# ScalarE and VectorE in hardware loops, GpSimd casting eight rows at a time, in a DMA-bound fused low-rank linear layer

## Chip, cores, metric

One core of a Trainium2 chip. The metric is device time in microseconds (us), median over executions. Every execution also has a span (first to last instruction of the kernel); the time is about 1.3 us above the span.

## The reference, cut

```python
x_flat = x.reshape(-1, in_dim)                 # x: 16 x 2048 x 256, float32
y = x_flat @ W                                 # W: 256 x 256
lora_out = ((x_flat @ lora_A) * lora_E) @ lora_B   # rank 16
y = y + scale * lora_out
```

Input and output are 33.55 MB each. The kernel folds the low-rank part into one weight matrix, so the work on x is one 256 x 256 product in bf16.

## The kernel before, the parts that matter

x stands in four chunks of 64 rows on each of 128 partitions. Three chunks have a place each in SBUF; the fourth is loaded over the first when that has been stored. One queue, issued by SyncE, carries all loads (`L`, chunk, first row, end) and stores (`S`) in this order:

```python
ORDER = [("A",), ("L",0,0,8), ("L",0,8,24), ("L",0,24,40), ("L",0,40,64),
         ("L",1,0,32), ("L",1,32,64), ("L",2,0,16), ("L",2,16,64),
         ("S",0,0,40), ("S",0,40,64), ("L",3,0,32), ("L",3,32,64),
         ("S",1,0,64), ("S",2,0,64), ("S",3,0,64)]
HELD = (2, 16)                 # GpSimd casts this row of chunk 2, and all behind it, only
HOLDERS = (("S", 0, 0, 40),)   # after this store has landed
```

A group is four rows (64 groups in all). GpSimd casts it to bf16, TensorE (PE) transposes it as pairs of bf16 words, VectorE (DVE) copies the transposed data out of PSUM, PE multiplies by the folded weights, ScalarE (ACT) copies the result over the rows that x came from. PE runs a hardware loop; the other engines' programs are written out:

```python
# GpSimd
for g in range(N_GROUPS):
    ... # waits for the load, and for the holder
    if g >= NS:
        gpsimd.wait_ge(s_turned, g - NS + 1)
    gpsimd.tensor_copy(out=stage[g % NS][:], in_=home(c)[:, b:b + CG, :]).then_inc(s_stage[g % UNROLL], 1)
# ScalarE
for g in range(N_GROUPS):
    scalar.wait_ge(s_y, g + 1)
    scalar.copy(out=home(c)[:, b:b + CG, :], in_=psum_y[g % NY][:]).then_inc(s_free[(g + NY) % UNROLL], 1)
    if g in ends:
        scalar.drain().then_inc(s_done, 1)      # releases a store
# VectorE
for g in range(N_GROUPS):
    vector.wait_ge(s_turned, g + 1)
    vector.tensor_copy(out=xt[g % NX][:], in_=psum_xt[g % NT][:].bitcast(BF16)).then_inc(s_xt[g % UNROLL], 1)
# PE
with tensor.Fori(0, N_GROUPS // UNROLL):
    for i in range(UNROLL):
        turn(i + 1, i)
        multiply(i)
# [cut: set-up, the end]
```

Of the kernel before, what the change touches and what calls it, by code (L numbers as in the profile page):

```python
# [7 lines left out]
P = 128  # L8
FP32 = mybir.dt.float32
BF16 = mybir.dt.bfloat16  # L10
# [3 lines left out]
ROWS = 64  # L14
N_CHUNKS = 4
N_HOMES = 3

ORDER = [
    ("A",),
    ("L", 0, 0, 8),  # L20
    ("L", 0, 8, 24),
    ("L", 0, 24, 40),
    ("L", 0, 40, 64),
    ("L", 1, 0, 32),
    ("L", 1, 32, 64),
    ("L", 2, 0, 16),
# [13 lines left out]
WARM_UP = 2  # L40

CG = 4
GPC = ROWS // CG
N_GROUPS = N_CHUNKS * GPC

NS, NX, NT, NY = 2, 2, 2, 2

UNROLL = 4
# [3 lines left out]
def kernel(  # L52
# [20 lines left out]
    y_chunks = out_flat.rearrange("(c p b) m -> c p b m", p=P, b=ROWS)  # L73

    sbuf, psum, sem = nc.alloc_sbuf_tensor, nc.alloc_psum_tensor, tc.alloc_semaphore
    homes = [sbuf(f"home{h}", [P, ROWS, K], FP32) for h in range(N_HOMES)]
    stage = [sbuf(f"stage{i}", [P, CG, K], BF16) for i in range(NS)]
    xt = [sbuf(f"xt{i}", [P, CG, P * KT], BF16) for i in range(NX)]
    ident = sbuf("ident", [P, P], FP32)

    w_sb = sbuf("w_sb", [P, KT, M], FP32)
    a_sb = sbuf("a_sb", [P, KT, R], FP32)
    b_sb = sbuf("b_sb", [R, M], FP32)
    e_sb = sbuf("e_sb", [R, 1], FP32)
    ate = sbuf("ate", [R, KT, P], FP32)
    weff = sbuf("weff", [P, KT, M], BF16)
    psum_xt = [psum(f"psum_xt{i}", [P, CG, P], FP32) for i in range(NT)]
    psum_y = [psum(f"psum_y{i}", [P, CG, M], FP32) for i in range(NY)]
# [8 lines left out]
    stored = {op: sem(f"stored_{op[1]}_{op[2]}") for op in ORDER if op in waited}  # L97
    stored_rest = nc.alloc_semaphore("stored_rest")
    n_rest = sum(op[0] == "S" and op not in waited for op in ORDER)
    ends = sorted((c * ROWS + e) // CG - 1 for kind, c, s, e in (op for op in ORDER if op[0] == "S"))  # L100
    s_ident = sem("ident_made")
    s_pe_set_up = sem("pe_set_up")
    s_ate = sem("ate_made")
    s_stage = [sem(f"staged{i}") for i in range(UNROLL)]
    s_turned = sem("turned")
    s_xt = [sem(f"xt_made{i}") for i in range(UNROLL)]
    s_y = sem("multiplied")
    s_free = [sem(f"y_free{i}") for i in range(UNROLL)]
    s_done = sem("rows_done")

    def home(c):
        return homes[c % N_HOMES]

    sync, gpsimd, scalar, vector, tensor = nc.sync, nc.gpsimd, nc.scalar, nc.vector, nc.tensor

# [19 lines left out]
    def sync_program():  # L135
        for n, op in enumerate(ORDER):
            if op[0] == "A":
                a = lora_A.rearrange("(q t) r -> q t r", t=KT)
                ins = sync.dma_start(out=a_sb[:], in_=a).then_inc(set_up_loaded["a"], 16)
                opening.append(ins.ins.name)  # L140
                continue
            kind, c, s, e = op
            at_home = home(c)[:, s:e, :]
            if kind == "L":
                for st in stored:
                    if st[1] == c - N_HOMES and st[2] < e and s < st[3]:
                        sync.wait_ge(stored[st], 16)
                ins = sync.dma_start(out=at_home, in_=x_chunks[c, :, s:e, :]).then_inc(loaded[op], 16)
                if n == 1:
                    opening.append(ins.ins.name)  # L150
            else:
                sync.wait_ge(s_done, ends.index((c * ROWS + e) // CG - 1) + 1)
                sync.dma_start(out=y_chunks[c, :, s:e, :], in_=at_home).then_inc(stored.get(op, stored_rest), 16)

    def gpsimd_program():
        gpsimd.memset(ident[:], 0.0).then_inc(s_ident, 1)  # L156
        gpsimd.wait_ge(s_ident, 1)
        gpsimd.affine_select(  # L158
            out=ident[:],
            in_=ident[:],  # L160
            compare_op=ALU.not_equal,
            fill=1.0,
            base=0,
            pattern=[[-1, P]],
            channel_multiplier=1,
        ).then_inc(s_ident, 1)
        for g in range(N_GROUPS):
            c, b = g // GPC, g % GPC * CG
            for op, landed in loaded.items():
                if op[1:3] == (c, b):  # L170
                    gpsimd.wait_ge(landed, 16)
            if (c, b) == HELD:
                for op in HOLDERS:
                    gpsimd.wait_ge(stored[op], 16)
            if g >= NS:
                gpsimd.wait_ge(s_turned, g - NS + 1)  # L176
            gpsimd.tensor_copy(out=stage[g % NS][:], in_=home(c)[:, b:b + CG, :]).then_inc(s_stage[g % UNROLL], 1)  # L177

        gpsimd.wait_ge(s_turned, N_GROUPS - NS + 1)
        gpsimd.drain().then_inc(s_stage[N_GROUPS % UNROLL], 1)  # L180

    def scalar_program():
        for name, to, of in (
            ("w", w_sb, W.rearrange("(q t) m -> q t m", t=KT)),
            ("b", b_sb, lora_B),
            ("e", e_sb, lora_E[:, None]),
        ):
            ins = scalar.dma_start(out=to[:], in_=of).then_inc(set_up_loaded[name], 16)
            opening.append(ins.ins.name)
        for g in range(N_GROUPS):  # L190
            c, b = g // GPC, g % GPC * CG
            scalar.wait_ge(s_y, g + 1)
            scalar.copy(out=home(c)[:, b:b + CG, :], in_=psum_y[g % NY][:]).then_inc(s_free[(g + NY) % UNROLL], 1)  # L193
            if g in ends:
                scalar.drain().then_inc(s_done, 1)  # L195

    def vector_program():
        vector.wait_ge(set_up_loaded["e"], 16)
        vector.wait_ge(s_pe_set_up, 1)
        vector.tensor_scalar(  # L200
            out=ate[:],
            in0=psum_y[0][:R, :KT, :P],
            scalar1=e_sb[:],
            scalar2=float(scale),
            op0=ALU.mult,
            op1=ALU.mult,
        ).then_inc(s_ate, 1)
        for g in range(N_GROUPS):
            vector.wait_ge(s_turned, g + 1)
            vector.tensor_copy(out=xt[g % NX][:], in_=psum_xt[g % NT][:].bitcast(BF16)).then_inc(s_xt[g % UNROLL], 1)  # L210
            if g == 0:
                vector.wait_ge(set_up_loaded["w"], 16)
                vector.wait_ge(s_pe_set_up, 2)
                vector.tensor_add(out=weff[:], in0=w_sb[:], in1=psum_y[1][:, :KT, :]).then_inc(s_free[0], 1)  # L214
                vector.drain().then_inc(s_free[1], 1)

    def tensor_program():
        def turn(i, result=None):
            words = stage[i % NS][:].bitcast(FP32)
            staged = s_stage[i % UNROLL]  # L220
            for b in range(CG):
                if b == 0:
                    tensor.wait_ge(staged, 1)
                if b == CG - 1 and result is not None:
                    tensor.wait_ge(s_free[result % UNROLL], 1)
                ins = tensor.transpose(psum_xt[i % NT][:, b, :], words[:, b, :], ident[:])  # L226
                if b == 0:
                    ins.then_inc(staged, -1)
            ins.then_inc(s_turned, 1)

        def multiply(i):
            turned, free = s_xt[i % UNROLL], s_free[i % UNROLL]
            for b in range(CG):
                for t in range(KT):
                    if b == t == 0:
                        tensor.wait_ge(turned, 1)
                    ins = tensor.matmul(  # L237
                        psum_y[i % NY][:, b, :],
                        xt[i % NX][:, b, t::KT],
                        weff[:, t, :],  # L240
                        start=(t == 0),
                        stop=(t == KT - 1),
                    )
                    if b == 0:
                        ins.then_inc((turned, free)[t], -1)
            ins.then_inc(s_y, 1)

        tensor.wait_ge(s_ident, 2)
        for i in range(WARM_UP):
            tensor.matmul(psum_y[1][:, :2, :], ident[:], ident[:, None, :].to_broadcast([P, 4, P]), start=True, stop=True)  # L250
        tensor.wait_ge(set_up_loaded["a"], 16)
        for t in range(KT):
            ins = tensor.transpose(psum_y[0][:R, t, :P], a_sb[:, t, :], ident[:])  # L253
        ins.then_inc(s_pe_set_up, 1)
        turn(0)
        tensor.wait_ge(set_up_loaded["b"], 16)
        tensor.wait_ge(s_ate, 1)
        for t in range(KT):
            ins = tensor.matmul(psum_y[1][:, t, :], ate[:, t, :], b_sb[:], start=True, stop=True)  # L259
        ins.then_inc(s_pe_set_up, 1)  # L260
        assert N_GROUPS % UNROLL == 0 and all(UNROLL % n == 0 for n in (NS, NX, NT, NY))
        with tensor.Fori(0, N_GROUPS // UNROLL):
            for i in range(UNROLL):
                turn(i + 1, i)
                multiply(i)

    def wait_for_stores(nc):
        nc.sync.wait_ge(stored_rest, 16 * n_rest).then_inc(stored_rest, -16 * n_rest)
# [44 lines left out]
```

## Time and profile before

| | before |
|---|---|
| time, median of 3 | 161.36 us (161.30 to 161.37) |
| time of the profiled execution | 162.84 us, span 161.5 us |
| data moved by the queue of x and y | 67.13 MB |

The profiled execution is 1.48 us slower than the median of the timed ones.

From the page of the kernel before: the span, the DMA engines' mean busy share and rate in 40 slices of the span, and the queues (packets, bytes, share of 16 engines' span).

```profile
span 161.5 us, 2024 instructions
...
DMA  7999999999999997998999999799799799699690
GB/s 253 405 438 452 402 452 446 446 406 446 394 548 414 402 390 337 477 467 371 420 459 440 406 446 536 319 519 471 308 503 487 308 503 503 292 503 503 292 519 16
...
q1 hardware_dynamic: 2304, 67.13, 97.2%
...
q14 instruction: 3, 0.02, 0.0%
```

The data queue is busy 97.2% of the span: the kernel is bound by its DMA engines. The last slice holds almost no traffic. Three packets of the queue that the page calls instruction (q14; instruction fetches below) share the engines with it: 8192 bytes and 0.31 us each in the trace, at 80.95, 86.49 and 102.70 us, each starting 3 to 4 ns before a data packet of its engine ends.

The issues of SyncE, the DMA queue's own row of the timeline, kernel before (start, length in us, engine, line, what, count):

```profile
0.00 0.38 SPq L139 DMA_DIRECT2D a_sb<-in_lora_A_dram  x1
0.43 4.95 SPq L148 DMA_DIRECT2D home<-in_x_dram  x8
27.66 9.87 SPq L153 DMA_DIRECT2D out_dram<-home  x2
75.94 7.69 SPq L148 DMA_DIRECT2D home<-in_x_dram  x2
83.68 35.34 SPq L153 DMA_DIRECT2D out_dram<-home  x3
```

Every store is issued long before the engines reach it: the first at 27.66 us, behind eight loads that keep the engines busy until about 62 us, the last at 119 us, behind two older ones that keep them busy until about 139 us.

The stages of the kernel before (busy us of each engine, granted clock, DMA share, rate):

```profile
core 0: us, PE busy (x) PEld busy (x) DVE busy (x) ACT busy (x) POOL busy (x), PEclk, DMA share, GB/s
...
27.00:60.00 33.00, 31.52 (x289) 29.12 (x288) 16.60 (x24) 24.18 (x25) 23.86 (x23) 1.00 1.04 438
60.00:76.00 16.00, 0.96 (x9) 0.61 (x7) 0.69 (x1) 1.71 (x2) 0.00 (x0) 0.64 0.93 398
...
80.00:118.00 38.00, 37.58 (x337) 34.37 (x335) 18.67 (x27) 28.73 (x29) 25.94 (x25) 0.98 1.04 448
118.00:161.50 43.50, 0.00 (x0) 0.00 (x0) 0.00 (x0) 0.63 (x1) 0.00 (x0) 0.55 0.90 390
```

PE stands still by design while GpSimd is held (60 to 76 us) and has finished 43 us before the end. The page's chain of waits nevertheless names PE:

```profile
DMA 36%; PE 34%; POOL 1%; ACT 1%; issue 0%; SPq 0%; ACTq 0%; POOLq 0%
```

That chain follows releases. PE released stores that then stood in the queue, so its 34% are not time that a faster PE would save.

### The profile page before, as it was taken

Reading aid. Unit: us, or ns where it says so; the run is one execution under the profiler, and the core shown is the slowest. Engines: PE = TensorE matmul, PEld = TensorE weight load, DVE = VectorE, ACT = ScalarE, POOL = GpSimd, SP = SyncE. Lnnn points to the kernel's source line nnn. Section 1 sums busy time; section 2 is a strip of 40 time slices with the busy share of each in tenths; the row PEclk is TensorE's granted clock in tenths of the full one; section 3 lists DMA queues with packets and bytes.
Section 4 is the critical chain, followed back from the end, with each engine's and each line's share of the span. In section 5 each row is a group of like instructions: output and inputs, shape, how many; then the busy total and the mean of one; then the engine's idle time right before and its main releaser. Section 6 shows DMA issues by size and latency. Waiting matters only on the chain.

```text
span 161.5 us, 2024 instructions
## 1 busy us (share of the span) xinstructions
PE 95.4 (59%) x782; PEld 83.4 (52%) x782; DVE 45.4 (28%) x66; ACT 66.1 (41%) x65; POOL 66.9 (41%) x70
## 2 busy tenths in 40 slices
PE   2988999969999990000899999999910000000000
PEld 1347999959999990000789989999900000000000
DVE  0141555535555550000155555555400000000000
ACT  3003677747777772000157777777730000000000
POOL 1516768577778840001578777788200000000000
PEclk9975999999999999555599999999996555555555
DMA  7999999999999997998999999799799799699690
GB/s 253 405 438 452 402 452 446 446 406 446 394 548 414 402 390 337 477 467 371 420 459 440 406 446 536 319 519 471 308 503 487 308 503 503 292 503 503 292 519 16
DMA packets 2515, 67.43 MB, mean 418 GB/s; under 512 B 448, under 2 KB 464, under 8 KB 592
## 3 DMA queue, kind: packets, MB, share of 16 engines
q1 hardware_dynamic: 2304, 67.13, 97.2%
q10 hardware_dynamic: 208, 0.28, 0.6%
q14 instruction: 3, 0.02, 0.0%
HBM read 33.85 MB, written 33.55 MB: 417 GB/s over the span
## 4 chain that ended last, share of the span: by engine, by line
DMA 36%; PE 34%; POOL 1%; ACT 1%; issue 0%; SPq 0%; ACTq 0%; POOLq 0%
DMA out_dram<-home 30%; PE psum_y L237 22%; PE psum_xt L226 12%; DMA home<-in_x_dram 6%; POOL stage L177 1%; ACT home L193 1%; ACTq L195 0%; SPq L308 0%; POOLq L176 0%; SPq L272 0%
## 5 line engine op out<-in xcount | busy, mean ns | idle before, releaser
L193 ACT COPY home<-psum_y 128x1024 f32<-128x1024 f32 x64 | 64.8, 1012 | 50.5 <-PE psum_y L237 50.5
L177 POOL CAST stage<-home 128x1024 bf16<-128x1024 f32 x64 | 66.2, 1042 | 44.8 <-DMA out_dram<-home 17.5
L237 PE MATMUL psum_y<-weff,xt 128*128 128x256 bf16 x512 | 69.6, 281 | 0.0
L210 DVE COPY xt<-psum_xt 128x1024 bf16<-128x1024 bf16 x64 | 44.3, 692 | 63.4 <-PE psum_xt L226 63.4
L237 PEld LDWEIGHTS psum_y<-weff,xt 128*128 128x128 bf16 x512 | 51.8, 101 | 6.5
L226 PE MATMUL psum_xt<-ident,stage 128*128 128x128 f32 x260 | 41.4, 283 | 19.3 <-POOL stage L177 19.0
L226 PEld LDWEIGHTS psum_xt<-ident,stage 128*128 128x128 f32 x260 | 31.5, 146 | 22.1 <-issue 20.7
L250 PE MATMUL psum_y<-ident 128*128 128x512 f32 x4 | 3.7, 1078 | 2.9 <-POOL ident L158 2.9
L250 PEld LDWEIGHTS psum_y<-ident 128*128 128x128 f32 x4 | 1.2, 324 | 3.9 <-POOL ident L158 2.9
L200 DVE TENSOR_SCALAR ate<-psum_y,e_sb 16x256 f32<-16x256 f32 x1 | 0.5, 472 | 6.9 <-PE psum_y L253 6.9
L193 ACT ACT_TABLE_LOAD x1 | 1.3, 1283 | 2.1 <-SPq L272 2.1
L259 PE MATMUL psum_y<-b_sb,ate 16*128 16x256 f32 x4 | 1.1, 400 | 0.0
L156 POOL MEMSET ident<- 128x128 f32 x1 | 0.2, 205 | 1.7 <-SPq L272 1.7
L253 PEld LDWEIGHTS psum_y<-ident,a_sb 128*16 128x16 f32 x2 | 0.2, 114 | 1.2 <-issue 1.2
L214 DVE TENSOR_TENSOR weff<-w_sb,psum_y 128x512 bf16<-128x512 f32 x1 | 0.7, 687 | 0.4 <-PE psum_y L259 0.4
L259 PEld LDWEIGHTS psum_y<-b_sb,ate 16*128 16x128 f32 x4 | 0.7, 184 | 0.2 <-issue 0.2
L158 POOL TENSOR_SCALAR_AFFINE_SELECT ident<-ident 128x128 f32<-128x128 f32 x1 | 0.3, 293 | 0.2 <-POOL ident L156 0.2
L253 PE MATMUL psum_y<-ident,a_sb 128*16 128x128 f32 x2 | 0.4, 273 | 0.0
L294 POOL MEMSET const-float32-0.0<- 128x1 f32 x1 | 0.1, 99 | 0.2 <-issue 0.2
L294 POOL MEMSET const-bfloat16-1.0<- 128x1 bf16 x1 | 0.1, 103 | 0.0
L294 POOL MEMSET const-uint8-127<- 128x1 uint8 x1 | 0.1, 103 | 0.0
L294 POOL MEMSET const-float32-1.0<- 128x1 f32 x1 | 0.1, 99 | 0.0
## 6 DMA issues: line engine op xcount, KB each, us to landing
home<-in_x_dram SPq DMA_DIRECT2D x4, 4096.0 KB, 25.1
home<-in_x_dram SPq DMA_DIRECT2D x3, 2048.0 KB, 13.8
home<-in_x_dram SPq DMA_DIRECT2D x1, 6144.0 KB, 58.9
out_dram<-home SPq DMA_DIRECT2D x1, 5120.0 KB, 48.3
home<-in_x_dram SPq DMA_DIRECT2D x1, 3072.0 KB, 20.7
out_dram<-home SPq DMA_DIRECT2D x1, 3072.0 KB, 46.0
home<-in_x_dram SPq DMA_DIRECT2D x1, 1024.0 KB, 5.4
w_sb<-in_W_dram ACTq DMA_DIRECT2D x1, 256.0 KB, 3.0
```

What stands on the lines that cost most here:

```text
L158: gpsimd.affine_select(out=ident[:], in_=ident[:], compare_op=ALU.not_equal, fill=1.0, base=0, pattern=[[-1, P]], channel_multiplier=1,).t ...
L177: gpsimd.tensor_copy(out=stage[g % NS][:], in_=home(c)[:, b:b + CG, :]).then_inc(s_stage[g % UNROLL], 1)
L193: scalar.copy(out=home(c)[:, b:b + CG, :], in_=psum_y[g % NY][:]).then_inc(s_free[(g + NY) % UNROLL], 1)
L200: vector.tensor_scalar(out=ate[:], in0=psum_y[0][:R, :KT, :P], scalar1=e_sb[:], scalar2=float(scale), op0=ALU.mult, op1=ALU.mult,).then_in ...
L210: vector.tensor_copy(out=xt[g % NX][:], in_=psum_xt[g % NT][:].bitcast(BF16)).then_inc(s_xt[g % UNROLL], 1)
L214: vector.tensor_add(out=weff[:], in0=w_sb[:], in1=psum_y[1][:, :KT, :]).then_inc(s_free[0], 1)
L226: ins = tensor.transpose(psum_xt[i % NT][:, b, :], words[:, b, :], ident[:])
L237: ins = tensor.matmul(psum_y[i % NY][:, b, :], xt[i % NX][:, b, t::KT], weff[:, t, :], start=(t == 0), stop=(t == KT - 1),)
L250: tensor.matmul(psum_y[1][:, :2, :], ident[:], ident[:, None, :].to_broadcast([P, 4, P]), start=True, stop=True)
L253: ins = tensor.transpose(psum_y[0][:R, t, :P], a_sb[:, t, :], ident[:])
L259: ins = tensor.matmul(psum_y[1][:, t, :], ate[:, t, :], b_sb[:], start=True, stop=True)
L294: nc = _bacc.Bacc("TRN2", target_bir_lowering=False, num_devices=1)
```

## The change

The intent: shorter instruction streams, by assumption with fewer instruction fetches on busy DMA engines, and fewer waits for counts that grow. ACT's and DVE's copies become hardware loops, which needs one `ring` tensor in place of three homes and waits for the constant 1, with PE taking the counts down again. GpSimd casts eight rows at once. The larger stage buffers are paid for by laying the set-up weights in `stage[1]`. Stores are released by PE's count, two groups later. One small copy stands ahead of ACT's loop, so that the loading of the activation table goes with it; before it took 1.28 us at 2.05 us, under the line of the group copies (L193). The diff, cut to its core:

```diff
+CAST = 2 * CG
-    homes = [sbuf(f"home{h}", [P, ROWS, K], FP32) for h in range(N_HOMES)]
-    stage = [sbuf(f"stage{i}", [P, CG, K], BF16) for i in range(NS)]
+    ring = sbuf("ring", [P, RING, K], FP32)
+    stage = [sbuf(f"stage{i}", [P, CAST, K], BF16) for i in range(NS)]
+    spare = stage[1][:].bitcast(FP32)...    # w_sb, b_sb, ate live here at the start
 # SyncE
-                sync.wait_ge(s_done, ends.index((c * ROWS + e) // CG - 1) + 1)
+                sync.wait_ge(s_done, (c * ROWS + e) // CG + NY)
 # GpSimd: 32 casts for 64
+            if n == 1:
+                gpsimd.wait_ge(s_weff, 1)
+            if n >= NS:
+                gpsimd.wait_ge(s_room, n - NS + 1)
+            gpsimd.tensor_copy(out=stage[n % NS][:], in_=rows(c, b, b + CAST)).then_inc(s_stage[n % NS], 1)
 # ScalarE
-        for g in range(N_GROUPS): ...
+        scalar.copy(out=one[:], in_=ident[:, :1])
+        for n in (RING, N_CHUNKS * ROWS - RING):
+            with scalar.Fori(0, n // (UNROLL * CG)) as lap:
+                for i in range(UNROLL):
+                    scalar.wait_ge(s_y[i], 1)
+                    to = ring[:, bass.ds(lap * (UNROLL * CG) + i * CG, CG), :]
+                    scalar.copy(out=to, in_=psum_y[i % NY][:]).then_inc(s_free[(i + NY) % UNROLL], 1)
 # VectorE
+        with vector.Fori(0, N_GROUPS // UNROLL):
+            for i in range(UNROLL):
+                g = i + 1
+                vector.wait_ge(s_turned[g % UNROLL], 1)
+                vector.tensor_copy(...)
 # PE, in multiply(i)
+            updates = {(0, 1): (s_xt[i % UNROLL], -1), (1, 0): (s_free[i % UNROLL], -1),
+                       (1, 1): (s_turned[i % UNROLL], -1), (2, 0): (s_y[(i - NY) % UNROLL], -1),
+                       (2, 1): (s_done, 1), (3, 1): (s_y[i % UNROLL], 1)}
 # [cut: set-up of the counts, the end]
```

## The prediction

> **What bounds the kernel now.** The DMA engines. The page's queue table gives the data queue (loads of x, stores of y) 97.2% of 16 engines' span, 67.13 MB in 161.5 us; the table of stages shows a DMA share near 1 and 437 to 448 GB/s from 12 to 60 us and from 80 to 118 us, then stores alone. Compute is off the path: PE is busy 59%, ACT 41%, POOL 41%, DVE 28%; PE stands still from about 62 to 77 us (GpSimd waits for the first store by design), and compute ends at 118.6 us. The chain of waits names PE for 34% because it follows releases, but the store released at 27.7 us then took 48.3 us behind queued loads, and the last store is issued at 119 us with older stores to move until about 139 us. PE's pace (1.31 us per four-row group) has 20 us of slack at the end, the first store some 30.
>
> Within the DMA the path is the slowest of the 16 engines. Single packets in the trace: each engine moves about 27 GB/s back to back, but 13 finish between 158.3 and 159.0 us, the others at 159.4, 159.9 and 161.07. The straggler was 1.2 us behind the first engine from 11 us on, 1.95 after 62 us, 2.8 after the load that ends at 93 us. That last step holds an instruction fetch: the instruction queue moves three 8 KB packets, at 80.95, 86.49 and 102.70 us, 0.31 us each. The second and the slowed x packet after it (0.54 us over normal) cost one engine 0.85 us, which fits the straggler's step.
>
> **What the change does.** Data transfers and their order stay. ACT's and DVE's streams shrink to loops (64 copies become 4 per lap), POOL's casts from 64 to 32. [...] PE already loops here without fetches. I expect all three gone, at worst one left (GpSimd's, late).
>
> It adds: a first cast of 8 rows (estimate 2.05 us for 1.04), so PE starts about 1 us later; a second cast waiting for the folded weights, whose scratch space is now in its buffer; 64 address updates plus branches on ACT ([...]within its 0.3 us idle[...]); stores released two groups (2.6 us) later by PE's count. All inside slack, worth zero. The small copy moves the 1.28 us table load, off the path either way.
>
> **Sum.** Straggler minus its fetch: -0.85 us. The ramp and the slow patch at 59 to 62 us (all engines about 0.8 us late) stay.
>
> Predicted: 160.6 us, range 159.6 to 161.6. Chances: faster by over 2% 0.03, within 2% 0.95, slower by over 2% 0.02.
>
> **What shows it right or wrong.** Right: no instruction packets inside the span; data queue still 67.13 MB; spread of engine ends from 2.8 to about 2 us; stores issued later but landings unmoved; PE groups of 1.3 to 1.5 us. Wrong: instruction packets from loop branches; a hole in the DMA row where a store came late.
>
> **What would make it wrong.** The straggler's lag may come from the profile or chance, so that timed runs gain nothing; [...]ACT's address updates would have to eat 20 us of slack to matter.

The sum has one term, -0.85 us, set against the 161.36 us of the time table: 160.51 us, put as 160.6 us. That a loop needs no fetches rests on PE's loop alone; beyond that it was assumption.

## The result, and the profile after

| | before | after |
|---|---|---|
| first measurement, median | 161.44 us (161.30 to 161.65, 6) | 162.06 us (161.77 to 162.67, 6) |
| ratio of the fast runs, 95% interval | | 1.0041 (1.002 to 1.0061) |
| three repeats, ratio | | 0.9984 (0.9947 to 1.0022), 0.9999 (0.9977 to 1.0021), 1.0006 (0.997 to 1.0041) |
| all executions, mean | 161.65 us (45) | 161.74 us (24) |
| profiled execution, span | 161.5 us | 160.8 us |

A ratio is the mean time of one kernel's fast runs over that of the other's of the same rounds, so not quite the ratio of the medians. The means of all executions differ by 0.09 us, with a standard error of about 0.10 us (worked out from the spread of the 45 and the 24 times). So the change does nothing that these runs can tell from zero, and a gain of 0.85 us lies far outside; the 0.4% of the first measurement did not come back in three repeats. The prediction of 160.6 us was wrong in either case.

From the page of the kernel after:

```profile
span 160.8 us, 2042 instructions
...
DMA  7999999999999997998999999998998998998990
GB/s 265 412 432 452 410 450 448 448 407 448 391 522 452 403 379 328 479 418 379 458 420 456 448 399 473 432 522 359 424 505 359 442 505 359 440 505 359 440 505 33
...
q1 hardware_dynamic: 2304, 67.13, 97.7%
...
q14 instruction: 1, 0.01, 0.0%
```

SyncE's issues after:

```profile
0.00 0.38 SPq L143 DMA_DIRECT2D a_sb<-in_lora_A_dram  x1
0.43 5.00 SPq L152 DMA_DIRECT2D ring<-in_x_dram  x8
29.29 10.06 SPq L157 DMA_DIRECT2D out_dram<-ring  x2
75.63 7.73 SPq L152 DMA_DIRECT2D ring<-in_x_dram  x2
83.40 35.89 SPq L157 DMA_DIRECT2D out_dram<-ring  x3
```

Stages after, and the chain of waits:

```profile
27.00:60.00 33.00, 31.34 (x288) 28.93 (x287) 16.59 (x24) 24.28 (x24) 20.82 (x12) 1.00 1.03 433
60.00:76.00 16.00, 1.46 (x14) 1.10 (x12) 0.70 (x2) 2.02 (x2) 0.28 (x1) 0.63 0.92 398
...
80.00:118.00 38.00, 37.70 (x339) 34.74 (x337) 19.36 (x28) 28.50 (x29) 22.72 (x12) 0.98 1.04 449
118.00:160.80 42.80, 0.00 (x0) 0.00 (x0) 0.00 (x0) 0.85 (x1) 0.00 (x0) 0.55 0.91 395
```

```profile
PE 35%; DMA 34%; POOL 2%; ACT 1%; issue 0%; ACTq 0%; SPq 0%; POOLq 0%
```

The costs that the change adds are where they were expected, inside slack. The first store is issued 1.6 us later (29.29 for 27.66) and still waits for the same loads; PE keeps its pace of 1.31 us per group; ACT still idles 0.30 us between copies in spite of its address updates; no hole opens in the DMA row. Three fetches became one, and the queue moves the same 67.13 MB. Two of ACT's copies before (L193) and two after (L204), each 1.31 us behind the other, with the idle time before each in brackets:

```profile
17.41 1.01 ACT L193 COPY home<-psum_y 128x1024 f32<-128x1024 f32 x1 [0.91 <-PE psum_y L237]
18.72 1.01 ACT L193 COPY home<-psum_y 128x1024 f32<-128x1024 f32 x1 [0.30 <-PE psum_y L237]
85.09 1.01 ACT L204 COPY ring<-psum_y 128x1024 f32 x1 [0.30 <-PE psum_y L258]
86.40 1.01 ACT L204 COPY ring<-psum_y 128x1024 f32 x1 [0.30 <-PE psum_y L258]
```

To see more, one has to go below the page, to the single DMA packets of the trace. Chained by their times (in the traces of before and after, nine packets in ten start within 12 ns of the end of the one before them on their engine), they give the 16 engines' ends. Worked out for every execution that has a trace, all in us; "late" is the last engine's lag behind the middle of the 16 at the end of the second load, of the load that ends near 62 us, of the last load (near 101 us) and at the end:

```
kernel            span    middle  late at: 10    62   101   end
before           161.51   158.73          0.96  1.67  2.44  2.34
before, again    159.88   158.47          0.38  0.21  0.93  0.91
after            160.84   158.58          0.76  1.34  1.91  1.88
after, again     160.29   158.68          0.59  0.89  1.22  1.18
after, third     160.31   158.83          0.43  0.56  0.64  0.98
after, fourth    160.26   158.40          0.59  0.71  0.97  1.37
```

The middle engine ends at 158.4 to 158.8 us in all of them. What differs is the last one, and it differs as much between two executions of one kernel (2.34 and 0.91) as between the kernels.

### The profile page after: what moved, and what is told of

Its sections match the earlier page's. It is cut to its first block, busy times and chain, and to the rows that moved or that the text cites. A ratio compares the mean times of both kernels' runs of the same rounds, so it can differ in the third digit from the quotient of the medians.

```text
span 160.8 us, 2042 instructions
## 1 busy us (share of the span) xinstructions
PE 94.9 (59%) x782; PEld 83.2 (52%) x782; DVE 46.1 (29%) x67; ACT 66.2 (41%) x66; POOL 61.1 (38%) x38
## 3 DMA queue, kind: packets, MB, share of 16 engines
q1 hardware_dynamic: 2304, 67.13, 97.7%
## 4 chain that ended last, share of the span: by engine, by line
PE 35%; DMA 34%; POOL 2%; ACT 1%; issue 0%; ACTq 0%; SPq 0%; POOLq 0%
DMA out_dram<-ring 29%; PE psum_y L258 23%; PE psum_xt L238 12%; DMA ring<-in_x_dram 6%; POOL stage L184 2%; ACT ring L204 1%; ACTq L204 0%; SPq L335 0%; POOLq L183 0%; SPq L299 0%
## 5 line engine op out<-in xcount | busy, mean ns | idle before, releaser
L204 ACT COPY ring<-psum_y 128x1024 f32 x64 | 64.8, 1012 | 50.5 <-PE psum_y L258 50.5
L184 POOL CAST stage<-ring 128x2048 bf16<-128x2048 f32 x32 | 60.4, 1893 | 49.2 <-DMA out_dram<-ring 18.3
L227 DVE COPY xt<-psum_xt 128x1024 bf16<-128x1024 bf16 x64 | 44.3, 692 | 63.0 <-PE psum_xt L238 63.0
L209 DVE TENSOR_SCALAR stage<-psum_y,e_sb 16x256 f32<-16x256 f32 x1 | 0.5, 472 | 6.9 <-PE psum_y L276 6.9
L284 PE MATMUL psum_y<-stage 16*128 16x256 f32 x4 | 1.1, 400 | 0.0
L218 DVE COPY xt<-psum_xt 128x1024 bf16<-128x1024 bf16 x1 | 0.7, 690 | 1.1 <-PE psum_xt L238 1.1
L221 DVE TENSOR_TENSOR weff<-stage,psum_y 128x512 bf16<-128x512 f32 x1 | 0.7, 686 | 0.4 <-PE psum_y L284 0.4
L284 PEld LDWEIGHTS psum_y<-stage 16*128 16x128 f32 x4 | 0.7, 184 | 0.2 <-issue 0.2
L198 ACT COPY one<-ident 128x1 f32<-128x1 f32 x1 | 0.2, 191 | 0.0
```

What stands on the lines that cost most here:

```text
L184: gpsimd.tensor_copy(out=stage[n % NS][:], in_=rows(c, b, b + CAST)).then_inc(s_stage[n % NS], 1)
L198: scalar.copy(out=one[:], in_=ident[:, :1])
L204: scalar.copy(out=to, in_=psum_y[i % NY][:]).then_inc(s_free[(i + NY) % UNROLL], 1)
L209: vector.tensor_scalar(out=ate, in0=psum_y[0][:R, :KT, :P], scalar1=e_sb[:], scalar2=float(scale), op0=ALU.mult, op1=ALU.mult,).then_inc(s ...
L218: vector.tensor_copy(out=xt[0][:], in_=psum_xt[0][:].bitcast(BF16)).then_inc(s_xt[0], 1)
L221: vector.tensor_add(out=weff[:], in0=w_sb, in1=psum_y[1][:, :KT, :]).then_inc(s_free[0], 1)
```

## Experiments

Theory F: the straggler among the DMA engines is made by an instruction fetch; take the fetches away and the end comes 0.85 us sooner. Rivals: N, the straggler is drawn anew at each execution and another engine is nearly as late, so that taking fetches away uncovers that one; L and C, the loops or the larger casts cost something.

### Both kernels again

Edit: none, for either.

> The kernel before, unchanged, against itself: what chance does, and what its other executions look like. All theories: ratio 1.00. Theory S (the profile on record of before was an unlucky execution, 1.4 us over its own median): a new profile shows a span near 160.1 us and a spread of the engines' last packets near 1.4 us, with the same three instruction packets. Theory F (fetches alone decide): span again near 161.5 us.

> The changed kernel again: all theories expect 1.003 to 1.006 if the loss on record is real; within 0.2% of 1 if it was chance. The profile: one instruction packet, late (near 127 us). Last packets of the engines: median again near 158.5 us as in before; any difference must sit in the slowest engine.

Measured: before against itself 0.9995 (0.9956 to 1.0034), 161.45 us; after 0.9984 (0.9947 to 1.0022), 161.46 us, against 161.54 us. The eleven runs of before in this job reach from 161.10 to 163.17 us, so the execution profiled first (162.84 us) was one of the slow tail. From the page of the kernel before, profiled again:

```profile
span 159.9 us, 2024 instructions
...
q1 hardware_dynamic: 2304, 67.13, 98.1%
...
q14 instruction: 3, 0.02, 0.0%
```

The same kernel, with the same three fetches, is 1.6 us shorter. The fetch of 85.75 us again costs its engine 0.85 us (0.31 us, and 0.54 us over normal in the packet behind it), but that engine was not late before it, and ends about 0.9 us after the middle. In the execution that the prediction was read from, the fetch fell on an engine that was already the last, by 0.96 us at 10 us and 1.67 us at 62 us. Starts of the 32 KB packets of these two engines, with what the packet behind the fetch took over normal:

```
before:         82.86 84.07 85.28 [fetch 86.49] 86.79(+0.54) 88.54 ... ends last, 161.07; the next at 159.85
before, again:  82.12 83.33 84.54 [fetch 85.75] 86.05(+0.54) 87.80 ... ends at 159.37; another last, at 159.38
```

In the first trace the whole 0.85 us could have been gained. In the second, which is nearer to the median, taking the fetch away gains nothing: an engine without a fetch ends 0.01 us later anyway.

### Loops written out, and four-row casts

```diff
 # unrolled: the kernel after, ACT's loop (and DVE's likewise) written out
-        for n in (RING, N_CHUNKS * ROWS - RING):
-            with scalar.Fori(0, n // (UNROLL * CG)) as lap: ...
+        for g in range(N_GROUPS):
+            i, at = g % UNROLL, g * CG % RING
+            scalar.wait_ge(s_y[i], 1)
+            scalar.copy(out=ring[:, at:at + CG, :], in_=psum_y[i % NY][:]).then_inc(...)
 # cast4: the kernel after, four rows to a cast
-CAST = 2 * CG
+CAST = CG
+            # and one count of s_room ahead, from the set-up's first product
```

> The changed kernel with ScalarE's and VectorE's loops written out as 64 copies (constant waits, counts by PE, 8-row casts kept). Theory L (the loops cost: where instruction fetches fall, or branches): back to the time of before, ratio 1.00, with two of the three fetches in the span again between 80 and 105 us. Rival C (the 8-row casts or the counts on PE cost): stays at about 1.004. My own theory on record (fetches are harmful) would expect it slower than the changed kernel by up to 0.5%.

> The changed kernel with GpSimd casting 4 rows at a time again (loops and counts kept). Rival C1 (the larger casts slow the DMA engine that ends last): ratio 1.00. Theory L: stays at about 1.004, with GpSimd's fetch back near 80 to 90 us.

Measured: 0.9999 (0.9961 to 1.0038) and 1.0012 (0.9972 to 1.0053). Neither part costs or gains anything that these runs show; in the same job the kernel after stood at 0.9984, so there was no loss left for either to explain. The fetches changed with the streams that were made longer: unrolled has two at 85.9 and 88.4 us and one at 124.6, four-row casts have a single one at 80.1 us. So the one left in the kernel after is GpSimd's, near 125 to 127 us, past the last instruction that the trace records for the kernel (120.8 us) but before the last store ends; it costs its engine 0.31 + 0.12 = 0.43 us.

### The changed kernel a third and a fourth time

> The changed kernel a third time. Theory N (no systematic difference: the time is the end of the slowest of 16 DMA engines, whose lag of 1 to 3 us is drawn anew at each execution): ratio within 0.3% of 1. If the loss of the first measurement is real: 1.003 to 1.006 again.

> The changed kernel a fourth time, for the pooled size of the difference. Theory N (no systematic difference; the last engine's lag is drawn anew): ratio between 0.997 and 1.003. In the profile one engine again moves its eight packets of the second chunk's store in about 2.57 us instead of 2.42 and ends 0.8 to 1.4 us after the middle of the 16.

Measured: 0.9999 (0.9977 to 1.0021) and 1.0006 (0.997 to 1.0041). Both are what theory N says of the time. But the end of the last engine is not chance alone, as the next runs show.

### Which engine ends when no fetch hits the last one

In every trace of both kernels one engine stores the second chunk slowly: 64 KB packets in 2.57 us instead of 2.42. Starts of the 64 KB packets of two engines in the trace of the fourth run of after, and in brackets by how much a packet took longer than the usual 2.42 us (27.1 GB/s), where that is over 0.06 us:

```
ends last, 159.76:     100.56(+0.17) 103.15(+0.15) 105.72(+0.15) 108.29(+0.16) 110.86(+0.16) 113.44(+0.15)
                       116.01(+0.08) 118.50(+0.20) 121.12 123.53 125.95 ... 157.34
4th from last, 158.76: 100.38 102.79 ... 119.69 122.11 [fetch 124.52] 124.83(+0.13) 127.37 129.78 ... 156.34
```

This engine ends at 159.4 to 159.9 us in the six traces of before and after (159.85, 159.38, 159.84, 159.78, 159.80 and 159.76, in the order of the table above): second to last in the first trace of each kernel, last or within 0.1 us of last in the other four. It is what a removed fetch uncovers. Does the place in HBM make it slow?

```diff
-                sync.dma_start(out=y_chunks[c, :, s:e, :], in_=at_home)...
+                sync.dma_start(out=y_chunks[{1: 2, 2: 1}.get(c, c), :, s:e, :], in_=at_home)...
```

> The changed kernel with the destinations of the second and third chunk's stores exchanged; wrong result on purpose. In every trace so far one engine moves its eight packets of the second chunk's store (about 100.6 to 121.2 us) in 2.57 us instead of 2.42, 1.25 us of lag. If the place in HBM does it, the slow packets move to the third chunk's store (about 120 to 140 us). If the rows in SBUF or the moment do it (rival), they stay at 100 to 121 us.

Measured: the slow packets stay at 100.2 to 120.8 us (one execution, 161.28 us; wrong result, as meant). The place in HBM is out.

```diff
+HELD_2, HOLDER_2 = (3, 32), ("S", 1, 0, 64)
+            if (c, b) == HELD_2:
+                gpsimd.wait_ge(stored[HOLDER_2], 16)
 # [cut: the semaphore of that store]
```

> The changed kernel with GpSimd's last 32 rows held until the second chunk's store has landed (about 121 us), so that the engines run no instructions from about 108 to 121 us and work again until about 133 us, during the third chunk's store. Theory R (one DMA engine stores slowly whenever the compute engines run instructions): its slow packets (2.57 us) lie at 100 to 108 and at 121 to 133 us, none between. Rival (the slow spell belongs to the second chunk's store): slow from 100 to 121 us and not after. Total time within 1%, as the last store still is issued before 139 us.

GpSimd's timeline in this run (start, length, what, idle before and its releaser):

```profile
99.19 1.89 POOL L187 CAST stage<-ring 128x2048 bf16<-128x2048 f32 x1 [0.73 <-PE psum_y L261]
121.80 3.73 POOL L187 CAST stage<-ring 128x2048 bf16<-128x2048 f32 x2 [20.71 <-DMA out_dram<-ring]
127.76 1.89 POOL L187 CAST stage<-ring 128x2048 bf16<-128x2048 f32 x1 [2.24 <-PE psum_y L261]
130.57 1.89 POOL L187 CAST stage<-ring 128x2048 bf16<-128x2048 f32 x1 [0.92 <-PE psum_y L261]
```

And its slow engine's packets:

```
100.23(+0.17) 102.82(+0.15) 105.38 107.80 110.21 112.63 115.04 117.45 119.88 122.29
124.71(+0.09) 127.22(+0.10) 129.73(+0.16) 132.31(+0.15) 134.88(+0.17) 137.47(+0.10) 139.98(+0.16)
```

The slow spell went where the instructions went: none from 105.4 to 124.7 us, then again until about 142 us (the last slow packet begins at 139.98 us, when the closing drains are still being recorded, until 141 us). The compute ended at 139 us, not at the 133 us forecast, so the last store was issued at 139.1 us and the engines ran dry for some tenths of a us (DMA share 0.38 from 140 to 142 us; middle engine's end 159.39 us); the one execution took 161.85 us. So the stores of one engine are slowed while the compute engines run instructions (by 0.09 to 0.17 us of 2.42 us a packet in this run); that the slow spell moves with them rests on this one execution and on the drains below. What slows it was not shown. Nor was it shown whether the measuring has a part in it: all executions, the timed ones too, carry a span and a clock, so none here was run without it.

### More fetches, late and early

Two kernels with 512 drains on the kernel after, behind the loops, while the last stores run. The drains are there only to make a stream longer:

```diff
 # drains_act512                         # drains_two256: 256 on each of ACT and DVE
+        for _ in range(512):
+            scalar.drain()
```

> The changed kernel with 512 empty drain instructions on ScalarE behind its last copy, while the last stores run: about 4 more instruction fetches of 8 KB from one stream, near 120 to 155 us. Theory D (one stream's fetches all queue at one DMA engine, each costing it 0.3 to 0.85 us): that engine ends 1.3 to 3.4 us later, and the time rises by 0.5 to 2.5 us (0.3 to 1.5%) since other engines' lag hides some. Rival (fetches are spread over the engines, or cost nothing at this point): time within 0.3% of 1, no engine later by over 1 us.

> The same 512 drains, split as 256 on ScalarE and 256 on VectorE: the same number of fetches in all. Theory D: two engines later by half as much each, 0.6 to 1.7 us, mostly hidden behind the slowest engine, so time up by 0 to 1 us, less than with all on ScalarE. Rival (cost depends on the number of fetches alone): same time as with 512 on ScalarE.

Measured: 1.0069 (1.004 to 1.0097) and 1.0068 (1.0041 to 1.0096), 162.75 and 162.77 us against 161.76 us. With all drains on ACT, its four fetches (124.6, 129.9, 135.3 and 140.7 us; a fifth at 146.3 us comes after the kernel's recorded end, as GpSimd's does in the kernel after) all lie in gaps of one engine's chain, with 0.15 to 0.25 us of excess behind each, which is theory D; but the split was not cheaper, which is against it. The packets say why: the drains also lengthen the slow spell, to 141 us and 132 us. With about 23 recorded instructions per us (a matmul and its weight load counted once; before and after have 12.9 and 13.3 from 80 to 118 us) most of its packets are 0.12 to 0.24 us over normal, with about 48 per us 0.22 to 0.36 us. In both kernels that engine ends last, at 160.90 and 160.88 us; the engine with ACT's fetches ends at 160.55 us. These two runs mix two causes, so a cleaner one followed: the drains early, where most fetches meet loads.

```diff
 # early: the kernel after, VectorE's loop written out
+        for g in range(1, N_GROUPS + 1):
+            vector.wait_ge(s_turned[g % UNROLL], 1)
+            vector.tensor_copy(...)
+            for _ in range(9):
+                vector.drain()
```

> The changed kernel with VectorE's copies written out again and nine empty drains behind each (576 in all), so that VectorE's stream needs about 5 fetches while loads and compute still run. Theory D (one stream's fetches all hit one DMA engine, 0.5 to 0.85 us each): that engine becomes the last one, 2.5 to 4 us later than the middle, and the time rises by 1 to 2.5 us. Rival (what slowed the kernels with drains at the end was only the longer slow spell of the engine that stores slowly): time up by less than 0.4 us, the fetches spread or hidden. PE's groups stay at 1.31 us in both.

Measured: 165.22 us against 161.43 us, ratio 1.0229 (1.0184 to 1.0273). From its page:

```profile
span 163.8 us, 2585 instructions
...
DMA  7999999999999989989999999997998899799760
...
q1 hardware_dynamic: 2304, 67.13, 95.8%
...
q14 instruction: 6, 0.05, 0.1%
```

Five of the six fetches are VectorE's, at 25.7, 44.2, 62.2, 98.8 and 116.6 us. The last engine's lag behind the middle is 1.1 us at 10 us, 3.2 us at 62 us, 4.2 us at 101 us and 4.9 us at the end, and it ends at 163.32 us, 2.8 us after the next. The middle still ends at 158.4 us, as in the kernels before and after. So fetches do cost, 0.8 to 1.0 us each in this run (0.92, 0.98, 0.83, 0.98 and 0.78 us, with the packet behind each), and those of one stream pile up on one engine. This is theory D; the rise of 3.8 us in time is more than the 2.5 us forecast as its top. The rival, under 0.4 us, is out.

## Why the prediction was wrong

- What binds: right. DMA engines busy 97%, compute in slack, within the DMA the slowest engine. No repeat contradicts it.
- What the change adds: right, worth zero. Pace 1.31 us per group, stores 1.6 us later for the 2.6 us forecast, an eight-row cast of 1.89 us for the 2.05 us estimated, ACT's updates within its 0.30 us of idle.
- Fetches: "all three gone, at worst one left (GpSimd's, late)" was right. One fetch at 0.85 us on its engine was right too; the early drains show such costs add up when they fall on one engine.
- The step that failed: "Straggler minus its fetch: -0.85 us", as a gain of the kernel's time. The fetch's cost to its engine was sized right; what was wrong is that the kernel would end earlier by it. Measured, the term is nothing: the mean of all executions after is 0.09 us above that of before, with a standard error of about 0.10 us. Two faults lie in it. First, the straggler was read from an execution of 162.84 us and subtracted from the median of other executions, 161.36 us, which ended 1.48 us sooner; on the time table both numbers stood side by side. For its own execution it would have given 162.84 - 0.85 = 161.99 us. Second, a last engine can be brought forward only to the next one. In the execution of 161.21 us the engine that the fetch hit ended at 159.37 us and the slowly storing one, which no fetch had hit, at 159.38 us: there the gain is 0.00 us, not 0.85. With the fetches gone, the slowly storing engine still ended at 159.76 to 159.84 us in all four traces of after.
- "The straggler's lag may come from the profile or chance" was listed as what would make it wrong. It did. The three repeats' medians (161.46, 161.65 and 161.64 us) lie at the upper edge of the range of 159.6 to 161.6 us; that they come so near says nothing for the term, as the kernel before lies there too (161.43 to 161.76 us in the same jobs).
- For the engine whose stream is fetched no stall was seen: in the kernel with early drains VectorE's copies stay 1.31 us apart around four of its five fetches (at the one of 62.2 us it stands still by design). In the time of before and after the fetch's cost was hidden too, but by other engines' lag, not because it is free to the data queue: 0.85 us on one engine.
- Open: why the first measurement gave 1.0041 with an interval that leaves out 1. Its job ran at another time; three later ones, on chips 8, 6 and 1, show nothing of it. Open too is what slows one engine's stores while instructions run, and what makes the lag in the first 10 us and near 60 us, where in the first two profiles the last engine fell behind before any fetch.

No version here beats both kernels. The slow spell moves with the compute, and compute that leaves one store meets another: with GpSimd held out of the second chunk's store, the slow packets came again from 124.7 us until about 142 us (one execution).

## What to carry to other kernels

This kernel, with its data queue busy 97.2% of 16 engines' span, ended with the slowest engine (161.07 us of a span of 161.5 us), so taking traffic off one engine could gain at most its lag behind the next to last: 1.22 us in that execution, 0.01 us in the next. Look for that lag first in a kernel bound the same way. Before costing a term read from one trace, compare that execution's time with the median of the timed ones, and if they differ by more than the effect, take a second trace. Keep the streams of busy kernels short all the same: nine empty instructions per group on one engine cost 2.3% here, through five fetches.

## What the traces show of fetches and engines

- Every fetch inside the spans of these traces is one packet of 8192 bytes, and VectorE's five in the kernel with early drains lie 121 to 138 recorded instructions apart.
- A fetch takes the DMA engine that carries it 0.31 us plus 0.10 to 0.54 us in the packet behind it (kernels before and after). In the kernel with early drains all fetches of VectorE's stream piled up on one engine, and that engine, 1.1 us behind the middle at 10 us, ended 4.9 us behind it after five.
- With the loops on PE, ACT and DVE no fetch occurred while they ran: one instruction packet in the span, at 127.1 us in the trace of the kernel after, whose compute ends at 119 us. There were three with ACT's and DVE's written out, at the same time (0.9984 and 0.9999 of the kernel before).
- The 16 engines together moved 430 to 435 GB/s in 33 of the 40 stretches of 4 us, loads and stores alike, in the traces of before and of after (a packet's bytes spread over its time; the views above count them all where the packet starts, hence up to 449 there). The last engine ended 0.9 to 2.3 us behind the middle in six executions of these two kernels.
- One engine stored 6% slower (2.57 us for 64 KB, not 2.42) while the compute engines ran instructions, in every trace of before and after.
